# The last two row groups of a cross-entropy kernel cut into thirteen other pieces, and one Ln moved up

## The chip, the cores and the metric

The kernel runs on one core of a Trainium2 chip. The metric is the device time in microseconds (us).

Some words used below: a *piece* is the part of a row group that one load brings in; a load *lands* when the last of its packets has been written; a kernel has *slack* where an engine would wait anyway, so that a delay there costs nothing. Ln is the natural logarithm.

## The reference

```
logits: 16 x 512 x 32000 float32, labels: 16 x 512 int32
m    = max(logits)                             # over the 32000 columns
lse  = log(sum(exp(logits - m))) + m
loss = lse - logits[label]                     # 8192 values
```

The kernel leaves out the maximum: it sums exp(logit) directly. The 8192 rows are 64 groups of 128 rows, one row per partition, and all 1048.6 MB of logits must be read once.

## The kernel before

`loads` is a list of (group, buffer, position in the buffer, columns). Three buffers of 16000 columns rotate. The sync engine issues each load. ScalarE takes the exponential in place and sums it (`accum_out`). GpSimd copies the label's logits out of the tile for most groups, and gathers them from memory for groups 0 and 61 to 63.

```
plan(0, [[4000, 4000, 8000], [16000]], [(0, 0), (0, 1), (0, 2), (1, 0)])
for g in range(1, G - 2):
    plan(g, [[W], [W]], [(0, 0), (1, 0)])                      # W = 16000
plan(G - 2, [[W], [10000, 6000]], [(0, 0), (1, 0), (1, 1)])
plan(
    G - 1,
    [[7400, 5840, 2260], [4540, 3720, 2920, 1780, 1460, 1120], [960]],
    [(0, 0), (0, 1), (1, 0), (1, 1), (1, 2), (0, 2), (1, 3), (1, 4), (1, 5), (2, 0)],
)
# ... (cut: tiles, label positions)
for j, (g, b, at, n) in enumerate(loads):
    # ... (cut: a new buffer)
    nc.sync.dma_start(out=t[:, at:at + n], in_=lg_pg[:, g, c0:c0 + n])
    # ... (cut: label pick)
    exp(g, t[:, at:at + n])
    # ... (cut)
    left = len(loads) - 1 - j
    if left == 6:
        nc.vector.reduce_sum(out=totals[:], in_=sums[:], axis=X)         # groups 0 to 62
        # ... (cut: label logits)
    if left == 4:
        nc.scalar.activation(out=logsum[:], in_=totals[:], func=LN)      # groups 0 to 62
        nc.vector.tensor_tensor(out=res[:], in0=logsum[:], in1=lab_logit[:, 0:G - 1], op=ALU.subtract)
    if left == 1:
        nc.vector.reduce_sum(out=part[:], in_=sums_last[:, 0:K - 1], axis=X)
nc.sync.dma_start(out=out_pg[:, 0:G - 1], in_=res[:])
nc.scalar.activation(out=logsum_last[:], in_=sums_last[:, K - 1:K], func=LN, bias=part[:])
nc.vector.tensor_tensor(out=res_last[:], in0=logsum_last[:], in1=lab_logit[:, G - 1:G], op=ALU.subtract)
nc.sync.dma_start(out=out_pg[:, G - 1:G], in_=res_last[:])
```

The softmax here doesn't subtract the row's maximum and nothing guards it: scores larger than these inputs give would overflow.

Of the kernel before, what the change touches and what calls it, by code (L numbers as in the profile page):

```python
# [20 lines left out]
def kernel(  # L21
# [10 lines left out]
    G = B * S // P  # L32
    W = 16000
# [9 lines left out]
    loads = []  # L43

    def plan(g, widths_by_buffer, order):

        n_buffers = 1 + max((l[1] for l in loads), default=-1)
        for b, i in order:
            ws = widths_by_buffer[b]
            loads.append((g, n_buffers + b, sum(ws[:i]), ws[i]))  # L50

    plan(0, [[4000, 4000, 8000], [16000]], [(0, 0), (0, 1), (0, 2), (1, 0)])
    for g in range(1, G - 2):
        plan(g, [[W], [W]], [(0, 0), (1, 0)])
    plan(G - 2, [[W], [10000, 6000]], [(0, 0), (1, 0), (1, 1)])
    plan(
        G - 1,
        [[7400, 5840, 2260], [4540, 3720, 2920, 1780, 1460, 1120], [960]],
        [(0, 0), (0, 1), (1, 0), (1, 1), (1, 2), (0, 2), (1, 3), (1, 4), (1, 5), (2, 0)],
    )  # L60
    assert sum(l[3] for l in loads) == G * V

    data = ctx.enter_context(tc.tile_pool(name="data", bufs=3))
# [100 lines left out]
    def exp(g, ap):  # L164
        k = n_exp.get(g, 0)
        n_exp[g] = k + 1
        s = sums[:, g, k:k + 1] if g < G - 1 else sums_last[:, k:k + 1]
        nc.scalar.activation(out=ap, in_=ap, func=EXP, accum_out=s)  # L168

    for j, (g, b, at, n) in enumerate(loads):  # L170
        if b not in buffers:
            buffers[b] = data.tile([P, W], FP32, tag="t", name="t")
        t = buffers[b]
        c0 = col.get(g, 0)
        col[g] = c0 + n
        nc.sync.dma_start(out=t[:, at:at + n], in_=lg_pg[:, g, c0:c0 + n])  # L176
        if g in picked:
            h = c0 // W
            i = picked.index(g) % NB
            if h == 0 and i == 0:  # L180
                pk = picks.tile([P, NB * 2, NI], FP32, tag="pk", name="pk")
            nc.gpsimd.indirect_copy(  # L182
                out=pk[:, 2 * i + h, :], data=t[:], idxs=lists[:, g, h, 0:3], i_know_this_is_slow=True
            )
        exp(g, t[:, at:at + n])
        if g in picked and h == 1 and i == NB - 1:
            nc.vector.copy_predicated(own[:], one_hot[:].unsqueeze(1).to_broadcast([P, NB * 2, NI]), pk[:])  # L187
            nc.vector.reduce_sum(  # L188
                out=found[:, :, g - NB + 1:g + 1].rearrange("p h g -> p g h"),
                in_=own[:].rearrange("p (g h) n -> p g h n", h=2),  # L190
                axis=X,
            )

        left = len(loads) - 1 - j
        if left == 6:
            nc.vector.reduce_sum(out=totals[:], in_=sums[:], axis=X)  # L196
            lo, hi = picked[0], picked[-1] + 1
            nc.vector.tensor_copy(out=lab_logit[:, lo:hi], in_=found[:, 1, lo:hi])
            nc.vector.copy_predicated(lab_logit[:, lo:hi], in_first[:, lo:hi], found[:, 0, lo:hi])  # L199
        if left == 4:  # L200
            nc.scalar.activation(out=logsum[:], in_=totals[:], func=LN)  # L201
            nc.vector.tensor_tensor(out=res[:], in0=logsum[:], in1=lab_logit[:, 0:G - 1], op=ALU.subtract)  # L202
        if left == 1:
            nc.vector.reduce_sum(out=part[:], in_=sums_last[:, 0:K - 1], axis=X)
# [36 lines left out]
```

## Time and profile before

| quantity | before |
|---|---|
| time, median of 3 runs | 2431.32 us (2431.27 to 2431.38) |
| load queue's share of the 16 DMA engines | 99.8% |
| ScalarE busy | 72% |
| last load packet ends (packet records) | 2424.88 us |
| last exponential starts / span ends | 2425.41 / 2429.5 us |

These are lines of the profile page of the kernel before: busy time by engine, the DMA queue of the loads (packets, MB, share of 16 engines) and the mean rate. DVE is VectorE, ACT is ScalarE, POOL is GpSimd.

```profile
DVE 22.9 (1%) x63; ACT 1748.9 (72%) x281; POOL 86.6 (4%) x132
...
q1 hardware_dynamic: 20304, 1048.62, 99.8%
...
HBM read 1048.64 MB, written 0.03 MB: 432 GB/s over the span
```

The loads fill the DMA engines from end to end, and ScalarE has a quarter of the span to spare. Only what follows the last load can become shorter, unless the loads themselves do. The Trainium skill, "DMA: Bandwidth & Descriptors", section "Where 436 GB/s comes from", gives a ceiling of 435.2 GB/s for the paths into the on-chip memory; the measured mean of 432 GB/s is just below it.

This is the end of the timeline of before (start in us, duration in us, engine, line, operation; in brackets the idle time before it and what ended that; L168 is line 168 of the kernel, and SPq the sync engine issuing a DMA):

```profile
2368.14 13.54 ACT L168 ACTIVATE t<-t 128x16000 f32<-128x16000 f32 x1 [5.28 <-DMA t<-in_logits_dram]
...
2418.92 2.09 ACT L168 ACTIVATE t<-t 128x2260 f32<-128x2260 f32 x1
2420.91 0.19 ACT L168 ACTIVATION_READ_ACCUMULATOR t<-t 128x1 f32 x1
2421.01 0.24 ACT L201 ACTIVATE logsum<-totals 128x63 f32<-128x63 f32 x1
2421.15 1.67 ACT L168 ACTIVATE t<-t 128x1780 f32<-128x1780 f32 x1
...
2425.41 1.00 ACT L168 ACTIVATE t<-t 128x960 f32<-128x960 f32 x1
2425.50 0.16 DVE L204 TENSOR_REDUCE part<-sums_last 128x1 f32<-128x9 f32 x1 [4.00 <-ACT t L168]
2426.32 0.19 ACT L168 ACTIVATION_READ_ACCUMULATOR t<-t 128x1 f32 x1
2426.54 0.29 ACT L208 ACTIVATE logsum_last<-sums_last,part 128x1 f32<-128x1 f32 x1
2426.87 0.16 DVE L209 TENSOR_TENSOR res_last<-logsum_last,lab_logit 128x1 f32<-128x1 f32 x1 [1.20 <-ACT logsum_last L208]
2427.05 0.34 SPq L210 DMA_DIRECT2D out_dram<-res_last  x1
```

From the last load packet (2424.88) to the end (2429.5) there are 4.6 us: 0.53 until the exponential starts, 1.00 for the exponential, then accumulator read, Ln, subtract, and the store. Each piece before it is sized so that ScalarE is done about when the next one lands.

The chain of waits of before, near its end (start, length, what):

```profile
2382.65 33.53 DMA t<-in_logits_dram
2416.18 0.02 issue
2416.20 4.90 ACT t L168 x4
2421.10 0.15 ACT logsum L201
2421.24 4.12 ACT t L168 x5
```

The profile follows the end back on ScalarE to the 2920-column piece at 2416.20, and from there to a load.

### The profile page before, as it was taken

The page shows a single profiled execution, that of the slowest core. Times are in us where ns is not written, and L with a number is a line of the kernel's source. Part 1 is how long each engine was busy: PE and PEld are TensorE (multiplying, and loading weights), DVE is VectorE, ACT ScalarE, POOL GpSimd, SP SyncE. Part 2 cuts the span into 40 slices and gives each one's busy share as a digit, 9 for nine tenths or more (in the row PEclk, how much of TensorE's full clock was granted, in tenths as well). Part 3 has the DMA queues.
Part 4 walks back from the last instruction along what each step waited for, and adds up shares of the span by engine and source line. Part 5 has one row for each costly group of instructions (what it writes and reads, how often), then busy time and mean ns, then how long its engine had stood idle before and what let it go on. Part 6 is the DMA issues. An engine that isn't in the chain of part 4 may idle for free.

```text
span 2429.5 us, 954 instructions
## 1 busy us (share of the span) xinstructions
DVE 22.9 (1%) x63; ACT 1748.9 (72%) x281; POOL 86.6 (4%) x132
## 2 busy tenths in 40 slices
DVE  0000000000000000000000000000000000000000
ACT  4777767777677767777677776777667776777769
POOL 0000000000000000000000000000000000000000
DMA  9999999999999999999999999999999999999998
GB/s 423 438 423 437 438 428 432 438 436 424 438 436 428 434 438 433 427 438 435 429 434 437 433 428 437 435 427 435 437 434 429 435 437 426 435 437 433 430 434 377
DMA packets 20583, 1048.74 MB, mean 432 GB/s; under 512 B 2656, under 2 KB 2784, under 8 KB 3296
## 3 DMA queue, kind: packets, MB, share of 16 engines
q1 hardware_dynamic: 20304, 1048.62, 99.8%
q10 hardware_dynamic: 144, 0.07, 0.0%
q14 instruction: 7, 0.06, 0.0%
q0 software_dynamic: 128, 0.00, 0.0%
HBM read 1048.64 MB, written 0.03 MB: 432 GB/s over the span
## 4 chain that ended last, share of the span: by engine, by line
DMA 73%; ACT 24%; issue 2%; POOL 1%; SPq 0%; POOLq 0%; DVE 0%; ACTq 0%
DMA t<-in_logits_dram 73%; ACT t L168 24%; POOL pk L182 1%; SPq L176 0%; POOLq L236 0%; ACT logsum_last L208 0%; DVE res_last L209 0%; ACT logsum L201 0%; POOLq L182 0%; ACTq L168 0%
## 5 line engine op out<-in xcount | busy, mean ns | idle before, releaser
L168 ACT ACTIVATE t<-t 128x16000 f32<-128x16000 f32 (+5 forms) x139 | 1734.8, 12481 | 676.7 <-POOL pk L182 635.7
L182 POOL INDIRECT_COPY pk<-t,lists 128x48 f32 x120 | 81.6, 680 | 2216.8 <-DMA t<-in_logits_dram 2216.8
L187 DVE COPY_PREDICATED own<-one_hot,pk 128x384 f32<-128x384 int32 x15 | 8.9, 593 | 2282.9 <-POOL pk L182 2282.9
L168 ACT ACTIVATION_READ_ACCUMULATOR t<-t 128x1 f32 x139 | 25.9, 186 | 0.0
L188 DVE TENSOR_REDUCE found<-own 128x8 f32<-128x384 f32 x15 | 8.3, 555 | 0.5
L114 POOL DMA_INDIRECT lab_logit<-in_logits_dram,idx x4 | 4.1, 1033 | 1.2 <-issue 0.9
L107 ACT ACT_TABLE_LOAD x1 | 1.3, 1283 | 1.2 <-PEq L225 1.2
L196 DVE TENSOR_REDUCE totals<-sums 128x63 f32<-128x315 f32 x1 | 0.5, 481 | 81.5 <-ACT t L168 81.5
L154 DVE TENSOR_SCALAR lists<-clamped,mine 128x64 uint16<-128x64 f32 x6 | 1.2, 364 | 0.0
L110 POOL TENSOR_TENSOR idx<-idx,labs 128x64 int32<-128x64 int32 x1 | 0.3, 318 | 7.5 <-DMA labs<-in_labels_dram 7.5
L202 DVE TENSOR_TENSOR res<-logsum,lab_logit 128x63 f32<-128x63 f32 x1 | 0.2, 225 | 24.9 <-ACT logsum L201 24.9
L157 DVE MEMSET own<- 128x384 f32 x1 | 0.4, 378 | 0.0
L140 DVE TENSOR_SCALAR one_hot<-entries,at_entry 128x48 int32<-128x48 f32 x1 | 0.3, 347 | 0.1
L129 DVE TENSOR_SCALAR mine_at<-mine 128x3 f32<-128x3 f32 x2 | 0.3, 170 | 0.1
L108 DVE MEMSET sums<- 128x315 f32 x1 | 0.3, 321 | 0.9 <-PEq L225 0.9
L132 DVE TENSOR_TENSOR mine<-mine,mine_at 128x3 f32<-128x3 f32 x2 | 0.3, 162 | 0.1
L208 ACT ACTIVATE logsum_last<-sums_last,part 128x1 f32<-128x1 f32 x1 | 0.3, 294 | 0.0
L125 DVE TENSOR_SCALAR mine<-part16f 128x1 f32<-128x1 f32 x3 | 0.3, 147 | 0.0
L135 DVE TENSOR_SCALAR mine_at<-mine 128x1 f32<-128x1 f32 x3 | 0.3, 147 | 0.0
L201 ACT ACTIVATE logsum<-totals 128x63 f32<-128x63 f32 x1 | 0.2, 238 | 0.0
L199 DVE COPY_PREDICATED lab_logit<-in_first,found 128x60 f32<-128x60 int32 x1 | 0.2, 231 | 0.0
L122 DVE TENSOR_SCALAR part<-part 128x1 int32<-128x1 int32 x1 | 0.2, 154 | 7.7 <-POOL part L111 7.7
(17 smaller groups left out, 2.7 us busy)
## 6 DMA issues: line engine op xcount, KB each, us to landing
t<-in_logits_dram SPq DMA_DIRECT2D x124, 8000.0 KB, 41.6
t<-in_logits_dram SPq DMA_DIRECT2D x1, 5000.0 KB, 35.9
t<-in_logits_dram SPq DMA_DIRECT2D x2, 2000.0 KB, 9.6
t<-in_logits_dram SPq DMA_DIRECT2D x1, 4000.0 KB, 21.3
t<-in_logits_dram SPq DMA_DIRECT2D x1, 3700.0 KB, 32.9
t<-in_logits_dram SPq DMA_DIRECT2D x1, 3000.0 KB, 42.7
t<-in_logits_dram SPq DMA_DIRECT2D x1, 2920.0 KB, 39.5
t<-in_logits_dram SPq DMA_DIRECT2D x1, 2270.0 KB, 26.4
```

What stands on the lines that cost most here:

```text
L107: nc.scalar.preload_act_table_set("natural_log_exp_and_others")
L108: nc.vector.memset(sums[:], 0.0)
L110: nc.gpsimd.tensor_tensor(out=idx[:], in0=idx[:], in1=labs32, op=ALU.add)
L114: nc.gpsimd.indirect_dma_start(out=lab_logit[:, g:g + 1], out_offset=None, in_=lg, in_offset=bass.IndirectOffsetOnAxis(ap=idx[:, g:g + 1], ...
L125: nc.vector.tensor_scalar(out=mine[:, q:q + 1], in0=part16f[:], scalar1=4.0 * q, scalar2=None, op0=ALU.add)
L154: nc.vector.tensor_scalar(out=lists[:, :, h, q], in0=clamped[:, h, :], scalar1=mine[:, q:q + 1], scalar2=None, op0=ALU.mult)
L157: nc.vector.memset(own[:], 0.0)
L168: nc.scalar.activation(out=ap, in_=ap, func=EXP, accum_out=s)
L182: nc.gpsimd.indirect_copy(out=pk[:, 2 * i + h, :], data=t[:], idxs=lists[:, g, h, 0:3], i_know_this_is_slow=True)
L187: nc.vector.copy_predicated(own[:], one_hot[:].unsqueeze(1).to_broadcast([P, NB * 2, NI]), pk[:])
L188: nc.vector.reduce_sum(out=found[:, :, g - NB + 1:g + 1].rearrange("p h g -> p g h"), in_=own[:].rearrange("p (g h) n -> p g h n", h=2), a ...
L196: nc.vector.reduce_sum(out=totals[:], in_=sums[:], axis=X)
```

## The change

The intent is to fit the sizes of the last pieces to two rates, that of the loads and that of ScalarE, so that the last piece can be smaller (745 columns instead of 960), and to have the Ln of the other 63 groups done earlier. Both kernels have 139 loads; the last two groups have thirteen pieces in both.

```diff
-    plan(G - 2, [[W], [10000, 6000]], [(0, 0), (1, 0), (1, 1)])
-    plan(
-        G - 1,
-        [[7400, 5840, 2260], [4540, 3720, 2920, 1780, 1460, 1120], [960]],
-        [(0, 0), (0, 1), (1, 0), (1, 1), (1, 2), (0, 2), (1, 3), (1, 4), (1, 5), (2, 0)],
-    )
+    b = loads[-1][1] + 1
+    for g, i, at, n in [
+        (G - 2, 0, 0, 12000), (G - 2, 1, 0, 11000), (G - 2, 2, 0, 9000),
+        (G - 1, 3, 0, 8720), (G - 1, 2, 9000, 6470), (G - 1, 3, 8720, 4700),
+        (G - 1, 4, 0, 3410), (G - 1, 3, 13420, 2550), (G - 1, 4, 3410, 1910), (G - 1, 4, 5320, 1455),
+        (G - 1, 4, 6775, 1135), (G - 1, 4, 7910, 905), (G - 1, 4, 8815, 745),
+    ]:
+        loads.append((g, b + i, at, n))
...
-        if left == 6:
+        if left == 9:
             nc.vector.reduce_sum(out=totals[:], in_=sums[:], axis=X)
...
-        if left == 4:
+        if left == 8:
             nc.scalar.activation(out=logsum[:], in_=totals[:], func=LN)
```

## The prediction

> **What bounds the kernel now.** The page gives queue q1 99.8% of the DMA engines' time at a mean 432 GB/s; ScalarE is busy 72%, VectorE 1%. The timeline shows full 16000-column exponentials starting 18.9 us apart while each takes 13.54 us, so ScalarE waits about 5.3 us for every load. The loads are the floor: 1048.6 MB at that rate is about 2420 us, and no load is added or removed (139 before and after). Only the uncovered end can change.
>
> **The end of before.** The packet records end the last load packet at 2424.9 us; the timeline starts the last exponential (960 columns) at 2425.41, and the span ends at 2429.5. The 4.6 us between are: about 0.5 of landing to start (the same 0.48 to 0.55 for each waiting piece), 1.0 exponential, accumulator read, 0.29 Ln, 0.16 subtract, issue of the store and 1.4 to its landing. Of this the change touches only the exponential.
>
> **What moves.**
> 1. The last piece shrinks from 960 to 745 columns. In the timeline an exponential costs 0.833 ns a column plus about 0.19 us (1.00 us at 960, 8.52 at 10000). The Trainium skill, "ScalarE: Activation LUTs", section "What ACT_TABLE_LOAD costs", states 186 ns + 0.833 N; the trace agrees. Gain: 215 x 0.833 ns = 0.18 us.
> 2. Each piece is sized so that ScalarE finishes it as the next lands. Loads take about 1.18 ns a column plus an estimated 0.04 to 0.075 us a piece (differences of landing ends in before). With 0.06 us, 905 columns cost ScalarE 0.95 us against 0.94 us for the next load: no slack left. In before the last piece started 0.03 us after its data allowed. Any error of the fit now adds up over seven pieces.
> 3. The Ln of 63 groups (0.24 us, delaying the next exponential by 0.14) moves from before 1780 columns to before 4700. In before the next piece's slack absorbed it (1460 columns started on its landing again). In after the pieces behind it have none, so roughly 0.1 us of it stays to the end. My chain of landings and exponentials, fitted to before, leaves the last exponential 0.03 to 0.3 us late.
> 4. Buffer reuse does not starve the loads: each new load is issued when at least 10 us of earlier loads are queued (estimate from the same rates).
> 5. The store of 63 groups is issued about 13 us earlier, behind the queued loads. In before, its packets show only as the load packets drain.
>
> **Sum.** -0.18 us from the smaller last piece, +0.03 to +0.3 us of ScalarE lateness in its place: about nothing. Predicted 2431.3 us, 8 in 10 between 2430.9 and 2431.8. Faster by over 2%: 0.01; same: 0.98; slower: 0.01.
>
> **What would show each step.** The last exponential taking 0.81 us (step 1). ScalarE's idle times before the pieces after the Ln vanishing, and the chain of waits running on ScalarE back to about the 4700-column piece instead of to the 2920-column piece (steps 2, 3). The last load packet ending within 0.2 us of 2424.9, DMA share staying near 1.0 until then (steps 4, 5).
>
> **What would make it wrong.** Loads slowed by the odd piece widths (row starts at multiples of 4 or 8 bytes, not 16)[...]; a stalled load queue; a larger cost per load piece than I think, which would give ScalarE slack and let the full 0.18 us through; the chip's spread.

## The result and the profile after

The changed kernel took 2431.1 us (median of 6 runs, 2430.98 to 2431.23), beside 2431.3 us (6 runs, 2430.98 to 2431.38) for the kernel before. The ratio is 0.9999, with a 95% interval of 0.9987 to 1.0012: the same.

The same lines of the page, for the changed kernel:

```profile
DVE 22.9 (1%) x63; ACT 1748.7 (72%) x281; POOL 86.7 (4%) x132
...
q1 hardware_dynamic: 20304, 1048.62, 99.8%
...
HBM read 1048.64 MB, written 0.03 MB: 432 GB/s over the span
```

Nothing there has moved. The end of the timeline has:

```profile
2404.92 5.59 ACT L170 ACTIVATE t<-t 128x6470 f32<-128x6470 f32 x1
2410.42 0.19 ACT L170 ACTIVATION_READ_ACCUMULATOR t<-t 128x1 f32 x1
2410.51 0.24 ACT L203 ACTIVATE logsum<-totals 128x63 f32<-128x63 f32 x1
2410.66 4.10 ACT L170 ACTIVATE t<-t 128x4700 f32<-128x4700 f32 x1
...
2424.47 0.94 ACT L170 ACTIVATE t<-t 128x905 f32<-128x905 f32 x1
2425.32 0.19 ACT L170 ACTIVATION_READ_ACCUMULATOR t<-t 128x1 f32 x1
2425.41 0.81 ACT L170 ACTIVATE t<-t 128x745 f32<-128x745 f32 x1
...
2426.13 0.19 ACT L170 ACTIVATION_READ_ACCUMULATOR t<-t 128x1 f32 x1
2426.35 0.29 ACT L210 ACTIVATE logsum_last<-sums_last,part 128x1 f32<-128x1 f32 x1
...
2426.86 0.34 SPq L212 DMA_DIRECT2D out_dram<-res_last  x1
```

The last exponential takes 0.81 us instead of 1.00, and everything behind it has moved up by 0.19 (the store is issued at 2426.86 instead of 2427.05). It starts at 2425.41 in both traces. The chain of waits now runs on ScalarE without a break from 2404.92, the 6470-column piece:

```profile
2404.92 5.69 ACT t L170 x2
2410.61 0.14 ACT logsum L203
2410.75 3.91 ACT t L170
2414.66 0.00 issue
2414.67 11.09 ACT t L170 x14
```

Two things must be separated here: how late ScalarE is after a load has landed, and when the loads land. I took the landings from the packet records of the traces: the end of the last of a load's 128 packets, on the clock of the span.

| piece of the changed kernel | landing | exponential starts | delay |
|---|---|---|---|
| 6470 | 2404.44 | 2404.92 | 0.48 |
| 4700 (behind the Ln) | 2410.08 | 2410.66 | 0.58 |
| 3410 | 2414.16 | 2414.76 | 0.60 |
| 2550 | 2417.25 | 2417.78 | 0.53 |
| 1910 | 2419.59 | 2420.10 | 0.51 |
| 745 | 2424.87 | 2425.41 | 0.54 |

The delay of a piece that ScalarE waits for is 0.47 to 0.55 us, in both kernels. The Ln makes the next two pieces about 0.1 us late, and two pieces later most of that is gone. In before the last piece's delay is 0.53. Since ScalarE has no pause from 2404.92 on, the last piece's 0.54 can hide a lateness of up to 0.07 us, but no more. So ScalarE all but keeps up, and step 1 (0.18 us predicted, 0.20 measured from the last exponential's start to the end of the span: 4.09 before, 3.89 after) should come through nearly whole.

But the loads of the last two groups became slower. The queue's packets fill 99.8% of the engines' time, so the packets' durations, summed and divided by 16 engines, are the time that these loads occupy the engines. They hardly depend on the run (76.64 in the repeat too). The last 64000 columns give:

| kernel | packets' time / 16 | last common landing to last load packet |
|---|---|---|
| before | 76.50 us | 76.20 us |
| after | 76.64 us | 76.34 us |

("Last common landing" is that of the last 16000-column load which both kernels have. For before it is inferred from the start of its exponential, less the delay of 0.55 us that such loads show.) So 0.14 us of the 0.20 went back to the loads. That the last exponential starts at 2425.41 in both traces is a coincidence of these two runs: the changed kernel's loads were 0.15 us ahead when the thirteen pieces began, by the chance of the run, and lost that lead in them. In the eight traces that have the same loads up to there, this landing lies anywhere from 2348.36 to 2348.86 us (inferred for before and x1, as above); that is as much as the spread of the timed runs.

### The profile page after: what moved, and what is told of

It reads as the page before. It is cut to its first block, busy times and chain, and to the rows that moved or that the text cites. A ratio compares the mean times of both kernels' runs of the same rounds, so it can differ in the third digit from the quotient of the medians. Undisturbed runs are those within 1.5% of the kernel's fastest.

```text
span 2429.3 us, 954 instructions
## 1 busy us (share of the span) xinstructions
DVE 22.9 (1%) x63; ACT 1748.7 (72%) x281; POOL 86.7 (4%) x132
## 3 DMA queue, kind: packets, MB, share of 16 engines
q1 hardware_dynamic: 20304, 1048.62, 99.8%
## 4 chain that ended last, share of the span: by engine, by line
DMA 72%; ACT 24%; issue 2%; POOL 1%; POOLq 0%; SPq 0%; DVE 0%; ACTq 0%
DMA t<-in_logits_dram 72%; ACT t L170 24%; POOL pk L184 1%; POOLq L238 0%; SPq L178 0%; ACT logsum_last L210 0%; DVE res_last L211 0%; ACT logsum L203 0%; POOLq L184 0%; ACTq L170 0%
## 5 line engine op out<-in xcount | busy, mean ns | idle before, releaser
L170 ACT ACTIVATE t<-t 128x16000 f32<-128x16000 f32 (+6 forms) x139 | 1734.8, 12481 | 676.8 <-POOL pk L184 635.4
L206 DVE TENSOR_REDUCE part<-sums_last 128x1 f32<-128x9 f32 x1 | 0.2, 162 | 14.5 <-ACT t L170 14.5
```

What stands on the lines that cost most here:

```text
L170: nc.scalar.activation(out=ap, in_=ap, func=EXP, accum_out=s)
```

## The experiments

My theory T was: the gain is the shorter last exponential and nothing else, ScalarE has no slack left behind the Ln, and a load piece costs the queue something for itself. The rivals: the difference is only spread (N); the moved Ln is the gain (L); the new sizes have slack left (F). Theory W came up with the table above: the odd widths slow the loads.

### Repeat, and each half of the change alone

`a0_after` is the changed kernel again. `x1_ln_up_alone` is the kernel before with:

```diff
-        if left == 6:
+        if left == 9:
...
-        if left == 4:
+        if left == 8:
```

`x2_pieces_alone` is the changed kernel with these two lines turned back. `x4_aligned` is the changed kernel with widths in multiples of 64 columns:

```diff
-        (G - 2, 0, 0, 12000), (G - 2, 1, 0, 11000), (G - 2, 2, 0, 9000),
-        (G - 1, 3, 0, 8720), (G - 1, 2, 9000, 6470), (G - 1, 3, 8720, 4700),
...
-        (G - 1, 4, 6775, 1135), (G - 1, 4, 7910, 905), (G - 1, 4, 8815, 745),
+        (G - 2, 0, 0, 12032), (G - 2, 1, 0, 10944), (G - 2, 2, 0, 9024),
+        (G - 1, 3, 0, 8704), (G - 1, 2, 9024, 6464), (G - 1, 3, 8704, 4672),
...
+        (G - 1, 4, 6784, 1152), (G - 1, 4, 7936, 896), (G - 1, 4, 8832, 768),
```

> The changed kernel again, five rounds beside the kernel before. Theory T (the gain is only the shorter last exponential, 215 columns at 0.833 ns = 0.18 us, with loads ending at the same time): median 0.1 to 0.25 us under the kernel before, last exponential 0.81 us. Rival N (the 0.2 us between the medians was the spread of single runs): the difference of the medians is under 0.1 us or changes sign.

> The old pieces, only the Ln of 63 groups moved up (behind the 5840-column exponential). Theory T: the next pieces wait for their loads anyway and absorb its 0.14 us, so the last exponential still starts about 0.5 us after the last load packet; time as before within 0.05 us. Rival L (the gain comes from moving the Ln): 0.1 to 0.2 us under the kernel before.

> The new pieces, the Ln left where it was (behind the 1910-column exponential). Theory T: the pieces behind it have no slack, so about 0.1 us of its 0.14 us reaches the end: last exponential 0.1 us later after the last load packet than in the changed kernel, time between the two kernels. Rival L (the move of the Ln is the whole gain): time as before. Rival F (the fit has slack): time as the changed kernel.

> The changed kernel with the thirteen widths rounded to multiples of 64 columns (256 bytes): 12032 to 768. In the changed kernel the loads of the last 64000 columns took 76.34 us (packet records, from the landing of the last common 16000-column load to the last load packet), in the kernel before about 76.19. Theory W (odd widths slow the loads): 0.1 us or more less than the changed kernel for those 64000 columns and for the total, despite 0.02 us more for the last exponential. Rival (width alignment does not matter): within 0.05 us of the changed kernel.

All four gave correct results (as did all later ones) and ran on one chip, five runs each, beside nine runs of the kernel before (median 2431.22, 2431.05 to 2431.34). "Delay" is from the last load packet to the start of the last exponential, "end" from that start to the end of the span, both in the profiled run.

| kernel | median us (range) | delay | end | packets' time / 16 |
|---|---|---|---|---|
| a0_after | 2431.12 (2430.97 to 2431.32) | 0.53 | 3.90 | 76.64 |
| x1_ln_up_alone | 2431.16 (2430.98 to 2431.37) | 0.53 | 4.08 | as before |
| x2_pieces_alone | 2431.38 (2431.13 to 2431.52) | 0.67 | 3.89 | 76.64 |
| x4_aligned | 2431.01 (2430.98 to 2431.12) | 0.55 | 3.91 | 76.55 |

For x1 the packets of the last 48000 columns, where the old pieces begin, give 57.59 us, and 57.58 in before.

Moving the Ln alone does nothing to the trace (delay 0.53, end 4.08), and its median moved by 0.06 us, well inside the run-to-run range: L falls. The new pieces with the Ln left late are the slowest of the four by the medians. T had put them between the two kernels, and rival L as before; the median is 0.16 us above before, with overlapping ranges, so only the trace decides here. These are lines of the timeline of x2_pieces_alone:

```profile
2422.15 0.19 ACT L170 ACTIVATION_READ_ACCUMULATOR t<-t 128x1 f32 x1
2422.24 0.24 ACT L203 ACTIVATE logsum<-totals 128x63 f32<-128x63 f32 x1
2422.38 1.40 ACT L170 ACTIVATE t<-t 128x1455 f32<-128x1455 f32 x1
...
2425.85 0.81 ACT L170 ACTIVATE t<-t 128x745 f32<-128x745 f32 x1
```

The Ln pushes the 1455-column piece back by 0.14 us, and the last piece still starts 0.67 us after its landing instead of 0.54. So the two halves belong together: the sizes leave no slack for an Ln among the small pieces, and the move takes it to where the wait for a load can still absorb most of it. By the trace, the new pieces alone would have been a small loss of 0.08 us: -0.20 (end), +0.14 (loads), +0.14 (delay).

The repeat gives -0.10 us by the medians. That agrees in sign with the first comparison (-0.2) and lies at T's lower edge, but the ranges overlap; timed runs alone do not exclude N. With the aligned widths the packets' time falls by 0.09 us (from the last common landing to the last load packet: 76.23 us instead of 76.34), and the median is the lowest of all kernels here, 0.21 us under before; its range overlaps that of the changed kernel, so the timed runs do not show that it is faster than that. The packets' time agrees with W; the last set of experiments tests W at 256 pieces instead of thirteen.

### The last piece, the slack, and the price of a load piece

`x3_last_2785` merges the last three pieces. `x5_ln_x8` repeats the Ln. `x6_gather_16` is the control for `x7_split_16`, which cuts 32 loads in mid-stream into 256.

```diff
# x3_last_2785 (with K = 8, and the Ln at the same piece)
-        (G - 1, 4, 6775, 1135), (G - 1, 4, 7910, 905), (G - 1, 4, 8815, 745),
+        (G - 1, 4, 6775, 2785),
# x5_ln_x8
-            nc.scalar.activation(out=logsum[:], in_=totals[:], func=LN)
+            for _ in range(8):
+                nc.scalar.activation(out=logsum[:], in_=totals[:], func=LN)
# x6_gather_16 (and x7)
-    gathered = [0, G - 3, G - 2, G - 1]
+    gathered = [0] + list(range(45, G))
-    sums = persist.tile([P, G - 1, 5], FP32)
+    sums = persist.tile([P, G - 1, 16], FP32)
# x7_split_16, in the loop over the groups, for 45 <= g < 61
+            plan(g, [[2000] * 8, [2000] * 8], [(b, i) for b in range(2) for i in range(8)])
```

> The last three pieces (1135, 905, 745) merged into one of 2785 columns. Theory T (the end pays 0.833 ns for each column of the last piece, less the load cost of the pieces saved): the last exponential takes 2.51 us instead of 0.81 (+1.70 us), the loads end 0.1 to 0.15 us earlier (two pieces fewer), so the time is about 1.5 us above the changed kernel. A rival in which the load stream alone sets the end: no change or slightly faster.

> The Ln of 63 groups done eight times in a row at its new place: about 7 x 0.14 = 1.0 us more of ScalarE time before the 4700-column piece. Theory T (no slack behind it): 0.85 to 1.0 us of it reaches the end, time about 0.9 us above the changed kernel. Rival F (the fit left slack in the later pieces): under 0.4 us reaches the end.

> Control for the next kernel: 16 groups (45 to 60) take their label logit by the indirect gather instead of the copy from the tile; loads as in the changed kernel. Expected within 1 us of the changed kernel (16 gathers of 128 four-byte packets).

> As the control, with the 32 loads of 16000 columns of groups 45 to 60 cut into 256 loads of 2000 columns (224 loads more), far from the end, loads still queued ahead. It measures the disputed cost of one more load piece in the stream. With the 0.04 to 0.075 us a piece of the prediction: 9 to 17 us above the control. If a piece cost nothing: 0. If a piece cost a stall of its own of 0.5 us or more: over 100 us.

| kernel | median us | last exponential starts | delay | end |
|---|---|---|---|---|
| before, same rounds | 2431.08 | - | - | - |
| x3_last_2785 | 2432.65 | 2425.11 | 0.47 | 5.74 |
| x5_ln_x8 | 2433.01 | 2427.32 | 2.47 | 3.89 |
| x6_gather_16 | 2432.33 | 2426.60 | 0.53 | 3.89 |
| x7_split_16 | 2449.43 | 2443.89 | 0.58 | 3.90 |

x3 is 1.57 us above before by the medians, and about 1.5 above the changed kernel (2431.12 on the other chip), as T said. Its last exponential:

```profile
2425.11 2.52 ACT L170 ACTIVATE t<-t 128x2785 f32<-128x2785 f32 x1 [1.80 <-DMA t<-in_logits_dram]
```

From the start of that exponential to the issue of the last store, x3 takes 3.17 us instead of 1.45: the last piece's length is paid at ScalarE's rate, in full. Its loads took 76.42 us of packets' time instead of 76.64, 0.11 us for each piece saved, and the delay was 0.07 us shorter. The end grew by 0.13 us more than the exponential accounts for (5.74 instead of 3.89), all of it after the store's last packet; the same 0.13 us comes back in y1 below, where it is traced.

In x5 I had the added time wrong. The timeline of x5_ln_x8:

```profile
2410.49 2.25 ACT L204 ACTIVATE logsum<-totals 128x63 f32<-128x63 f32 x8
2412.64 4.10 ACT L170 ACTIVATE t<-t 128x4700 f32<-128x4700 f32 x1
...
2427.32 0.81 ACT L170 ACTIVATE t<-t 128x745 f32<-128x745 f32 x1
```

Eight Ln operations into one tile took 2.25 us, 0.28 each, not 0.14. The 4700-column piece started at 2412.64 instead of 2410.66, 1.98 us later, and the last piece's delay grew by 1.93 us (2.47 instead of 0.54). Nearly all of it reaches the end: all pieces from 4700 down have together some 0.05 to 0.1 us of slack. F falls.

x7 is 17.1 us above its control for 224 more loads: 0.076 us for each (17.1 / 224). That is the top of the 0.04 to 0.075 us in the prediction, and would explain why the new sizes have just enough slack: with 0.076 us instead of 0.06, the time between landings is 0.016 us longer for each piece, or 0.11 us over the seven pieces behind the 4700-column one (an estimate from these two numbers). The changed kernel's own landings agree: the eight loads behind the 6470-column piece (16810 columns) took 20.43 us (2404.44 to 2424.87), where the prediction's 1.18 ns a column and 0.06 us a piece give 20.32. The control itself cost 1.2 us over before, a little more than expected.

### Widths again, at 256 pieces, and two more savings

`x8_split_256B` and `x9_split_odd` are x7 with other widths. `y1_first_whole` is x4 with the first group in two pieces. `y2_ln_scaled` is y1 with the last subtract folded into the Ln (loss = Ln(sum x exp(-label logit))).

```diff
# x8_split_256B, x9_split_odd: widths of a buffer's eight pieces
-                        [2000] * 8
+x8:                     [2048] * 7 + [1664]
+x9:                     [2001] + [2002] * 6 + [1987]
# y1_first_whole
-    plan(0, [[4000, 4000, 8000], [16000]], [(0, 0), (0, 1), (0, 2), (1, 0)])
+    plan(0, [[W], [W]], [(0, 0), (1, 0)])
# y2_ln_scaled, besides that
+        if j == 10:
+            nc.scalar.activation(out=inv_last[:], in_=lab_logit[:, G - 1:G], func=EXP, scale=-1.0)
...
+            nc.vector.tensor_tensor(out=part_inv[:], in0=part[:], in1=inv_last[:], op=ALU.mult)
...
-    nc.scalar.activation(out=logsum_last[:], in_=sums_last[:, K - 1:K], func=LN, bias=part[:])
-    nc.vector.tensor_tensor(out=res_last[:], in0=logsum_last[:], in1=lab_logit[:, G - 1:G], op=ALU.subtract)
+    nc.scalar.activation(out=res_last[:], in_=sums_last[:, K - 1:K], func=LN, bias=part_inv[:], scale=inv_last[:])
```

> As x7_split_16, but the small pieces are 2048 columns (seven of 2048 and one of 1664 to a buffer), so every row starts and ends on a multiple of 256 bytes. In x7 (2000 columns, row starts on multiples of 64 bytes) the time was 17.1 us above the control, 0.076 us a piece. Theory W (a row off a 256-byte boundary costs extra time in its packet): 1 to 4 us less than x7. Rival (only the count of pieces matters): as x7 within 0.5 us.

> As x7_split_16, but the pieces are 2001, six of 2002, and 1987 columns, so almost every row starts on an odd multiple of 4 bytes. Theory W, from the 3 to 4 ns a packet by which the odd-width packets of the changed kernel exceed those of the kernel before: 256 pieces x 8 packets of one engine x 2 to 4 ns = 4 to 8 us above x7. Rival (only the count matters): as x7 within 0.5 us.

> The aligned widths of x4_aligned, and the first group loaded in two pieces of 16000 columns instead of 4000, 4000, 8000 and 16000. Theory: two load pieces fewer at 0.076 us (measured by x7) end the load stream 0.15 us sooner and ScalarE has slack for the late start: 2430.75 to 2430.95 us. Rival (the first pieces hide a slow start of the stream): as x4 or slower.

> As y1_first_whole, and the final subtract goes: the last Ln is taken of (sum x exp(-label logit)), with scale and bias operands made before the end, and writes the loss itself. Takes the 0.16 us subtract and one hand-over (about 0.03 us) from the end and adds about 0.09 us to the Ln for its scale operand (estimate; the Ln with a bias operand took 0.29 us): 0.05 to 0.15 us under y1. If the end does not lie on that chain: as y1.

| kernel | median us | before, same rounds |
|---|---|---|
| x7_split_16 (from above) | 2449.43 | 2431.08 |
| x8_split_256B | 2452.11 | 2431.12 |
| x9_split_odd | 2452.18 | 2431.12 |
| y1_first_whole | 2431.16 | 2431.12 |
| y2_ln_scaled | 2431.11 | 2431.12 |

Both sides lose on the widths. (x8 and x9 ran on another chip than x7, but the kernel before differs by only 0.04 us between the two.) Rows on 256-byte boundaries were 2.7 us slower than rows of 8000 bytes, not faster, so W in the form I had given it (a row off a 256-byte boundary costs extra) falls. But the same number of pieces took 2.7 us more in x9 too, so the count is not all that matters either: against x6, a piece cost 0.088 to 0.089 us at these widths, where x7 has 0.076. The packet records agree in direction: the eight rows of a buffer took 2442 ns together in x7 (8 x 305.2), 2453 in x8 (7 x 313.8 + 256.8) and 2458 in x9 (306.3 + 6 x 308.1 + 303.1). What stays: the width of a row changes the time of its packet by a few ns that its size does not explain, and at the changed kernel's widths that is to its disadvantage. Which property of the width does it stays open.

y1 did not deliver its 0.15 us: the landing of the last 16000-column load is at 2348.55 us in y1 and 2348.54 in x4, and the packets of the first group took 38.68 us over 16 engines against 38.75 and 38.69 in x4 and the changed kernel. The 0.076 us of a load piece in mid-stream was not to be had at the start; why is open. Besides, y1's end is 4.04 us, where x4 has 3.91 with the same code. The two traces agree to 0.01 us up to the last packet of the last store; the 0.13 us arise after it. The semaphore records show where: at the end of the kernel the sync engine checks the completion semaphores one after another, about 0.06 us each. From the last store's own on, three checks are left in x4 and five in y1. All three kernels with 137 loads (x3, y1, y2) have five, and all those with 139 or 363 loads have three. So most of the 0.15 us between the medians of y1 and x4 has nothing to do with the loads. y2 did shorten the end. These are lines of the timeline of y1:

```profile
2425.34 0.82 ACT L170 ACTIVATE t<-t 128x768 f32<-128x768 f32 x1
...
2426.80 0.34 SPq L212 DMA_DIRECT2D out_dram<-res_last  x1
```

And of y2:

```profile
2425.27 0.83 ACT L172 ACTIVATE t<-t 128x768 f32<-128x768 f32 x1
...
2426.22 0.39 ACT L215 ACTIVATE res_last<-sums_last,part_inv,inv_last 128x1 f32<-128x1 f32 x1
2426.63 0.34 SPq L216 DMA_DIRECT2D out_dram<-res_last  x1
```

The store is issued 1.36 us after the last exponential's start, against 1.46 in y1 (2425.34 to 2426.80). The Ln grew from 0.29 to 0.39 us and the subtract went. The medians of y1 and y2 are 0.05 us apart with overlapping ranges, so this 0.1 us is shown in the trace and not in the timed runs. Nothing here beats x4_aligned, and no version is clear of the spread. The folded subtract was not tried with x4's 139 loads, where it would not carry the two further checks.

## Why the prediction was right or wrong

- **The bound.** Right: the load queue fills 99.8% of the DMA engines in both kernels, and the change could only act at the end. (1048.6 MB at 432 GB/s is 2427 us, not "about 2420"; nothing rests on it.)
- **Step 1, the shorter last exponential.** Right: 0.81 us instead of 1.00; the end after its start fell from 4.09 to 3.89 us. x3 shows the same in the other direction. The rate is that of the Trainium skill, "ScalarE: Activation LUTs", section "What ACT_TABLE_LOAD costs" (186 ns + 0.833 ns a column, which makes an estimate of 0.81 us for 745; the trace has 0.81).
- **Steps 2 and 3, no slack, and a late Ln that reaches the end.** The mechanism was right and the size too large. "Leaves the last exponential 0.03 to 0.3 us late" and "roughly 0.1 us of it stays to the end" came out as a delay of 0.54 us, 0.01 more than before and at most 0.07 above the shortest wait of 0.47. No run has the new pieces without any Ln, so how much of its 0.14 us is left at the end is not measured more closely. The mis-sized term is the cost of a load piece: I took 0.06 us, x7 measured 0.076, and the last eight landings took 0.11 us longer than my rates give. The prediction had named this as a risk. That there is next to no slack was right: x5's 1.98 us arrived as 1.93, and x2's 0.14 as 0.13. That the larger price of a piece is what kept the lateness so small follows from these rates; no run tests it alone. The prediction expected the chain of waits to run on ScalarE back to about the 4700-column piece; it reached one piece further, the 6470.
- **Step 4, no starved loads.** Right: in the view of windows, the stretch from 2300 to 2424 us has a DMA share of 0.99 and 423 GB/s in both kernels (the two figures at the end of each line, before first, then the changed kernel; ahead of them stand the busy times of three engines and the clock):

```profile
2300.00:2424.00 124.00, 2.19 (x6) 102.67 (x30) 0.68 (x1) 1.00 0.99 423
```

```profile
2300.00:2424.00 124.00, 2.19 (x6) 102.49 (x30) 0.68 (x1) 1.00 0.99 423
```

- **Step 5, the early store.** Right in effect: it waits behind the loads, 14.5 us to landing instead of 4.0 (below). It was issued 10.5 us earlier, at 2411.03 instead of 2421.53; the prediction said 13.
- **The sum.** 2431.3 was predicted and 2431.1 measured, inside the range. It is composed otherwise than predicted: -0.20 us from the last exponential, +0.14 from slower loads, +0.01 of lateness, together -0.05, where the prediction had -0.18 and up to +0.3 of lateness. The slower loads stood there only among the things that could make it wrong ("Loads slowed by the odd piece widths"). So that the sum came out near nothing is in part luck: the lateness that was to eat the gain hardly came, and a cost of about the same size that was not in the sum took its place. The timed differences, -0.2 and -0.10 by medians, are somewhat larger than -0.05; that is within the range of single runs (the loads before the changed part alone scatter by 0.5 us), and I do not explain it further.

The lines on the two stores, from the DMA view of before (out<-in, engine, count, KB, us from issue to landing):

```profile
out_dram<-res SPq DMA_DIRECT2D x1, 31.5 KB, 4.0
```

and of the changed kernel:

```profile
out_dram<-res SPq DMA_DIRECT2D x1, 31.5 KB, 14.5
```

The Trainium skill, "DMA: Bandwidth & Descriptors", section "Queues, rings and completion order", says that each DMA engine takes a ring's descriptors in order. This agrees, as far as the records go (they do not name the engine of a packet): the store was issued 14 us before the last load landed, and its packets ran from 2422.67 to 2424.99 us, while the last load packets drained. In before they ran from 2422.38 to 2425.00, though that store was issued 10.5 us later.

## What to carry to other kernels

When one resource is full from end to end, ask first how long the part behind its last piece of work is: here it was 4.6 of 2431 us, and the change could touch 0.2 of them. Tapering the last pieces trades the last piece's compute time against a price per piece (0.076 to 0.089 us in the load queue here, about 0.19 on ScalarE), and the fit ends when the two engines go in step; any operation placed among those pieces is then paid almost in full, so it has to go where the engine still waits. At such sizes judge by distances inside the trace, since the spread of the timed runs is as large as the effect, and look at each stretch of the end by itself: here a change in the number of loads alone moved the last checks by 0.13 us.

## What the Trainium skill lacked or had wrong

- "DMA: Bandwidth & Descriptors", section "Anatomy of one DMA": it fits about 2.0 us of fixed time to one (software-generated) DMA. It has no figure for one more DMA in a queue that is kept full from the sync engine; here that was 0.076 us (x7 against x6, 17.1 us for 224 loads), and 0.088 to 0.089 at the widths of x8 and x9.
- The same page, "How a descriptor splits into AXI transactions": by its account the bytes fetched before the start of a row that is not on a 256-byte boundary cost extra beats. Here 8192-byte rows on such boundaries were slower in total than 8000-byte rows that mostly were not (2452.11 against 2449.43 us, 256 pieces each), so boundaries alone do not predict the cost.
- "ScalarE: Activation LUTs", "What ACT_TABLE_LOAD costs": a further pointer operand adds about 93 ns; y2 agrees (Ln 0.39 us instead of 0.29). It says that back-to-back operations overlap by about 93 ns; that held between the Ln and the exponential behind it (0.24 us long, the next starts 0.14 to 0.15 after it), and not between eight Ln operations that write the same tile (0.28 us each; in x5 each starts about 0.03 us after the one before has ended).
- In the pages on DMA and on ScalarE I found no single figure for the time from the last packet of a load to the start of a ScalarE operation that waits for it (the DMA page has about 0.1 us for the semaphore update alone, in its account of the GpSimd path): 0.47 to 0.55 us here.
